# Modulation work spread over more stages, and split activations moved by a part of 128 bytes, in a two-layer hybrid flow step on one Trainium2 core

## The chip, the cores and the metric

The kernel runs on one core of one Trainium2 chip. The metric is the device time of one execution in microseconds (us). TensorE does the matrix products, VectorE and ScalarE the elementwise work, SyncE issues all DMAs; GpSimd does next to nothing here.

## What is computed

128 context tokens and 256 latent tokens (384 in all, three blocks of 128) pass through two layers of a hybrid backbone, everything in float32. Cut to what matters:

```python
def trunk_layer(x, mod, s0f, s0b, lp):                  # twice, DEPTH = 2
    shift1, scale1, gate1, shift2, scale2, gate2 = jnp.split(mod, 6, axis=-1)
    h = rms_norm(x, lp['g_norm1']) * (1 + scale1) + shift1
    z, xbc, dt_raw, p, u, v, gate_logits = jnp.split(h @ lp['w_in'], offs, axis=-1)
    y_ssd, s_f, s_b = ssd_mixer(z, xbc, dt_raw, s0f, s0b, ...)   # conv, SiLU, chunked scan both ways
    y_pool = pool_mixer(p, lp['w_pool'], lp['pool_scale'])       # windows of 2, 4, 8, 16 tokens
    y_gmlp = chunk_gmlp(u, v, lp['g_sgu'], lp['w_spatial'], lp['b_spatial'])  # v = rms_norm(v) first
    g_a, g_b, g_c = jnp.split(jax.nn.sigmoid(gate_logits), N_BRANCH, axis=-1)
    merged = (g_a * (y_ssd @ lp['w_br_ssd']) + g_b * (y_pool @ lp['w_br_pool'])
              + g_c * (y_gmlp @ lp['w_br_gmlp']))
    x = x + gate1 * (merged @ lp['w_out'])
    h2 = rms_norm(x, lp['g_norm2']) * (1 + scale2) + shift2
    f_gate, f_up = jnp.split(h2 @ lp['w_ffn_in'], 2, axis=-1)
    x = x + gate2 * ((jax.nn.silu(f_gate) * f_up) @ lp['w_ffn_out'])
...
    mod_ctx = (jax.nn.silu(c_ctx) @ w_ada[l] + b_ada[l]).reshape(1, 1, -1)   # adaLN modulation
    mod_lat = (jax.nn.silu(c) @ w_ada[l] + b_ada[l])[:, None, :]
```

D_MODEL is 1024, the SSD has 2048 channels in 32 heads, the FFN 2816. At the end comes one more RMSNorm, and the final scan states of the context tokens are returned too.

## The kernel before

**Split products.** TensorE works on a rounded form of float32 (`fp32r`). Each operand is split in a high part, rounded, and a low part, the rest; a product is three matmuls, high by high, high by low, low by high. There are two forms. In `mm3` (lines 165 to 167) the stationary operand is a 128x128 piece of the weights (`whi`, `wlo`), and the activations of all 384 tokens move; a unit of 1024 inputs is 24 such matmuls. In `opt_b`, called through `block_b` and `tiles_b` (lines 454 to 456), the stationary operand is a 128-token block of the activations and 512 columns of the weights move. The activations lie split in SBUF: `hthi`/`htlo` (the normalized input of all projections of a stage), `yh`/`yl` (the SSD's output), and pairs `ah`/`al` that `hl()` hands out from 16 buffers (pooled, mixed and gMLP values, which move; the merged values and the FFN's products, which are stationary in `opt_b`).

**Weights as a stream.** The class `Flow` holds a list of units in program order, each with its weight chunks. A chunk is 512 KB, one DMA into one of six raw buffers (128x1024). For a weight ScalarE casts it to `whi` (line 115), VectorE subtracts to get `wlo` (line 116); three chunks are split ahead. TensorE's order is the order of the list. On the other engines a scheduler orders the instructions by the priorities of program order, the split casts put a little ahead.

**Modulation.** The adaLN vectors of sections 2 to 5 of layer 0 and all six of layer 1 are 80 chunks ("ada") in the same stream. They need no TensorE: `ada` (line 289) has VectorE multiply each raw chunk by a row of SiLU(c), once for the context and once for the latent row, and sum along it (line 299, tile `ajunk`). The rows `crow` come from `silu_rows` (line 280), which stands at the end of the first front. After a section's eighth chunk `ada_end` transposes the result.

**Stages, per layer.** Front: the gMLP's `v` is projected, its statistics taken, and it is kept in HBM. SSD: dt, convolutions over B, C and x (`conv_unit`, tiles `cin`, `ca`, `th`, `bt`, `ct`), z, 16 pairs of heads with their scan, and as fillers between them the gMLP's `u` and the merge gates. Mixers: the order string `6745g23g1g0gAgB` names eight pool units (digits), late gate units (g) and the two group products of the pool's weights (A, B); then 8 units of the pool branch (brp) with the spatial gating between them, 8 of the gMLP branch (brg). Back: the output projection (out), the second norm, the first FFN units (fb), gate and up units (fi), and the FFN's output (fo) in two halves. The modulation chunks stand thus in the stream: 8 in each SSD stage, one after every second step in the mixers (16 per layer), 24 in the FFN of layer 0 and 8 in that of layer 1. In the mixers `mix_open` loads `v` back (`k<-vd`), and VectorE multiplies it by its reciprocal root mean square (tile `k`, factor `ssy`).

Of the kernel before, what the change touches and what calls it, by code (L numbers as in the profile page):

```python
# [19 lines left out]
D = 1024  # L20
# [20 lines left out]
HL = 16  # L41
WPRI = 1
# [13 lines left out]

ADA_S, ADA_M, ADA_F = 2, 2, 1
# [65 lines left out]
class Net:  # L123
# [67 lines left out]
    def build(self):  # L191
# [20 lines left out]
        self.hthi = b.tile([128, KT, TOK], F32R, name="hthi")  # L212
        self.htlo = b.tile([128, KT, TOK], F32R, name="htlo")
# [66 lines left out]
    def silu_rows(self):  # L280

        for n in range(2):
            c = self.crow[:, n, :]
            th = self.t(self.pool, "k4", [128, D], 4)
            self.act(th, c, ACTF.Tanh, scale=0.5)
            self.stt(c, th, 1.0, c, ALU.add, ALU.mult)
            self.ts(c, c, 0.5, ALU.mult)

    def ada(self, l, sec):

        hold = {}
# [12 lines left out]

        return [([("ada", l, sec, k)], step(k)) for k in range(KT)]

    def take(self, us):

        if us:
            self.flow.add(*us.pop(0))  # L310
# [169 lines left out]
    def front0(self):  # L480
# [84 lines left out]
        F.add([], self.silu_rows)  # L565
# [10 lines left out]
    def ssd(self, l):  # L576
# [4 lines left out]
        ada = self.ada(l, 2)  # L581

# [8 lines left out]
        for g in range(4):  # L591
# [7 lines left out]
            for t in range(4 * g, 4 * g + 4):  # L599
# [5 lines left out]
                if (t + 1) % ADA_S == 0:  # L605
                    self.take(ada)
# [9 lines left out]
        while ada:  # L616
            self.take(ada)
# [314 lines left out]
    def mixers(self, l):  # L932
# [3 lines left out]
        ada, count = self.ada(l, 3) + self.ada(l, 4), [0]  # L936

        def more():
            count[0] += 1
            if count[0] % ADA_M == 0:  # L940
                self.take(ada)

# [117 lines left out]
    def branch(self, l, br, c, w, src):  # L1060
# [13 lines left out]
        h = self.mg[c] = self.hl()  # L1074
# [37 lines left out]
    def back(self, l):  # L1112
# [19 lines left out]
        ada = self.ada(l, 5) + (self.ada(l + 1, 0) + self.ada(l + 1, 1) if l + 1 < DEPTH else [])  # L1132

# [14 lines left out]
        for half, kn in enumerate((6, 5)):  # L1148
            for f in range(at, at + 2 * kn - (0 if half else 2)):
# [3 lines left out]
                for _ in range(ADA_F + (f % 4 == 0)):  # L1153
                    self.take(ada)
                self.main([("fi", l, NF + f)], lambda w, f=f: self.ffn_up(l, f, w))
            at = 12
            if half == 0:
                F.add([], lambda: setattr(self, "rows", self.gate_rows(l, 1)))
            for q in range(2):
                spans = (1,) * (kn - KL) + (KL,) if half and q else (1,) * kn  # L1160
# [3 lines left out]
                self.block_b([("fo", l, q, r) for r in range(r0, r0 + kn)], spans, lambda k, r0=r0: self.fa[2 * r0 + k], after, mid, last)  # L1164
# [28 lines left out]
    def ffn_up(self, l, f, w):  # L1193
# [4 lines left out]
        h = self.fa[f] = self.hl()  # L1198
# [174 lines left out]
```

## Time and profile before

| | |
|---|---|
| median of 3 runs (lowest, highest) | 1877.2 us (1876.57, 1879.7) |
| profiled execution, its span | 1876.65 us, 1874.9 us |
| TensorE busy | 1831.0 us (98%) |
| VectorE busy | 1451.4 us (77%) |
| ScalarE busy | 965.1 us (51%) |
| DMA, mean | 182 GB/s, 341 MB |

By the trace the stages lie at: front of layer 0 until 67 us, its SSD 67 to 490, mixers 490 to 636, out and fb to 690, FFN to 955; layer 1: front to 1000, SSD to 1407, mixers to 1551, out to 1605, FFN to 1866, end 1875. A matmul's record lasts longer than the distance to the next one, since they are pipelined: a rate is read from start to start. A wait is the idle time of an engine just before an instruction, put down to what released it.

### The profile page before, as it was taken

How to read it: one execution, taken by the hardware profiler on the slowest of the kernel's cores; microseconds unless marked ns; L12 is line 12 of the kernel's file. 1: busy time of each engine (PE TensorE's matmuls, PEld its weight loads, DVE VectorE, ACT ScalarE, POOL GpSimd, SP SyncE). 2: the span in 40 equal slices, each digit the busy share in tenths (PEclk: the TensorE clock that was granted, in tenths of full speed). 3: DMA queues.
4: the chain of work that ended last, by engine and by line, in shares of the span. 5: the costliest groups of instructions: out<-in, count | busy, mean ns of one | idle time of the engine just before them, and what ended most of it. 6: DMA issues, size and time to landing. Idle time of an engine off the chain costs nothing.

```text
span 1874.9 us, 28980 instructions
## 1 busy us (share of the span) xinstructions
PE 1831.0 (98%) x10724; PEld 1730.5 (92%) x10724; DVE 1451.4 (77%) x2899; ACT 965.1 (51%) x1910; POOL 0.2 (0%) x4
## 2 busy tenths in 40 slices
PE   7989999999999999999999999999999899999998
PEld 4889999999999979989889999999999898998997
DVE  4699979998888787486458989799979887843545
ACT  4677767675342353323355977675833334432332
POOL 0000000000000000000000000000000000000000
PEclk9999999999999999999999999999999999999999
DMA  8756464644766655556445646455457674554431
GB/s 332 248 189 219 150 200 130 210 139 136 262 210 221 213 160 186 170 192 200 124 166 193 211 165 198 149 174 181 135 172 247 222 254 135 192 172 131 124 124 45
DMA packets 112293, 341.15 MB, mean 182 GB/s; under 512 B 12948, under 2 KB 38420, under 8 KB 112024
## 3 DMA queue, kind: packets, MB, share of 16 engines
q1 hardware_dynamic: 112152, 339.30, 55.8%
q8 instruction: 84, 1.38, 0.3%
q14 instruction: 57, 0.47, 0.1%
HBM read 314.38 MB, written 24.87 MB: 181 GB/s over the span
## 4 chain that ended last, share of the span: by engine, by line
PE 82%; DVE 11%; DMA 5%; issue 2%; ACT 1%; SPq 0%; DVEq 0%; ACTq 0%
PE ps_mm L165 19%; PE ps_mm L166 19%; PE ps_mm L167 19%; PE ps_mm L456 5%; PE ps_mm L455 5%; PE ps_mm L454 5%; DMA raw<-w 3%; PE ps_y L875 3%; DVE ajunk L299 2%; DVE wlo L116 2%; DVE ptree L147 1%; DMA k<-vd 1%; PE ps_st L840 1%; DVE t L150 1%; DVE accx L147 1%
## 5 line engine op out<-in xcount | busy, mean ns | idle before, releaser
L115 ACT CAST whi<-raw 128x1024 fp32r<-128x1024 f32 x394 | 412.9, 1050 | 535.6 <-PE ps_mm L166 224.0
L165 PE MATMUL ps_mm<-hthi,whi 128*128 128x384 f32 x1936 | 663.0, 342 | 1.4 <-ACT arg L144 1.4
L116 DVE TENSOR_TENSOR wlo<-raw,whi 128x1024 fp32r<-128x1024 f32 x394 | 481.5, 1223 | 231.8 <-ACT whi L115 227.5
L167 PE MATMUL ps_mm<-hthi,wlo 128*128 128x384 f32 x1936 | 655.0, 338 | 2.1 <-DVE wlo L116 2.1
L166 PE MATMUL ps_mm<-htlo,whi 128*128 128x384 f32 x1936 | 655.0, 338 | 0.0
L165 PEld LDWEIGHTS ps_mm<-hthi,whi 128*128 128x128 f32 x1936 | 364.8, 188 | 4.1 <-ACT arg L144 1.8
L167 PEld LDWEIGHTS ps_mm<-hthi,wlo 128*128 128x128 f32 x1936 | 364.4, 188 | 2.5 <-DVE wlo L116 2.5
L166 PEld LDWEIGHTS ps_mm<-htlo,whi 128*128 128x128 f32 x1936 | 364.7, 188 | 0.3
L299 DVE CUSTOM_DVE_ANT_0 ajunk<-raw,crow 128x1024 bf16<-128x1024 f32 x160 | 195.8, 1224 | 53.9 <-DMA raw<-w 53.0
L456 PE MATMUL ps_mm<-whi,al 128*128 128x512 f32 (+1 forms) x360 | 140.3, 390 | 0.0
L454 PE MATMUL ps_mm<-whi,ah 128*128 128x512 f32 (+1 forms) x360 | 140.0, 389 | 0.0
L455 PE MATMUL ps_mm<-wlo,ah 128*128 128x512 f32 (+1 forms) x360 | 139.2, 387 | 0.0
L150 DVE SCALAR_TENSOR_TENSOR ca<-cin,cw,ca 128x388 f32<-128x388 f32 x192 | 118.8, 619 | 2.1
L165 PE MATMUL ps_mm<-ah,whi 128*128 128x384 f32 x288 | 100.3, 348 | 11.3 <-ACT ah L159 8.1
L159 ACT CAST ah<-t 128x384 fp32r<-128x384 f32 x72 | 36.8, 511 | 124.9 <-DVE t L150 64.8
L166 PE MATMUL ps_mm<-al,whi 128*128 128x384 f32 x288 | 99.0, 344 | 1.1 <-DVE al L147 1.1
L167 PE MATMUL ps_mm<-ah,wlo 128*128 128x384 f32 x288 | 98.5, 342 | 0.0
L165 PE MATMUL ps_mm<-yh,whi 128*128 128x384 f32 x256 | 86.8, 339 | 0.0
L166 PE MATMUL ps_mm<-yl,whi 128*128 128x384 f32 x256 | 86.1, 336 | 0.0
L167 PE MATMUL ps_mm<-yh,wlo 128*128 128x384 f32 x256 | 86.1, 336 | 0.0
L455 PEld LDWEIGHTS ps_mm<-wlo,ah 128*128 128x128 f32 x360 | 67.6, 188 | 14.7
L456 PEld LDWEIGHTS ps_mm<-whi,al 128*128 128x128 f32 x360 | 67.6, 188 | 14.4
(234 smaller groups left out, 2454.3 us busy)
## 6 DMA issues: line engine op xcount, KB each, us to landing
raw<-w SPq DMA_DIRECT2D x474, 512.0 KB, 4.1
fb<-fsd SPq DMA_DIRECT2D x32, 768.0 KB, 4.8
thd<-spill SPq DMA_DIRECT2D x48, 192.0 KB, 2.4
spill<-thd SPq DMA_DIRECT2D x48, 192.0 KB, 4.5
araw<-wa SPq DMA_DIRECT2D x16, 512.0 KB, 5.7
s<-s SPq DMA_DIRECT2D x32, 128.0 KB, 2.2
so<-so SPq DMA_DIRECT2D x32, 128.0 KB, 2.5
k<-gd SPq DMA_DIRECT2D x8, 512.0 KB, 5.4
```

The source lines that it names most:

```text
L115: self.nc.scalar.copy(out=hi, in_=raw)
L116: self.nc.vector.tensor_tensor(out=lo, in0=raw, in1=hi.bitcast(F32), op=ALU.subtract)
L147: self.nc.vector.tensor_tensor(out=out, in0=a, in1=b, op=op)
L150: self.nc.vector.scalar_tensor_tensor(out=out, in0=a, scalar=s, in1=b, op0=op0, op1=op1)
L165: mm(out, lhsT=whi, rhs=xhi, start=first, stop=False)
L166: mm(out, lhsT=whi, rhs=xlo, start=False, stop=False)
L167: mm(out, lhsT=wlo, rhs=xhi, start=False, stop=last)
L299: self.nc.vector.tensor_tensor_reduce(out=junk, in0=raw, in1=self.crow[:, n, :], scale=1.0, scalar=0.0, op0=ALU.mult, op1=ALU.add, accum_o ...
L454: mm(out, lhsT=xh[:, ts], rhs=hi[:, ws], start=(kk == 0), stop=False)
L455: mm(out, lhsT=xh[:, ts], rhs=lo[:, ws], start=False, stop=False)
L456: mm(out, lhsT=xl[:, ts], rhs=hi[:, ws], start=False, stop=(kk == kn - 1))
L875: mm(o, lhsT=lt, rhs=rt, start=(n == 0), stop=(n == steps - 1))
```

## The change

The change has five parts.

1. **Modulation chunks.** One queue, `adaq`, holds all 80 in order, and stages take from it. In the SSD of layer 0 it is 12 instead of 8, in that of layer 1 8 as before; in the mixers of layer 0 one at each of the five `g` steps and one after each brg unit, 13 instead of 16; in those of layer 1 8, none before brg; in the FFN of layer 0 35 instead of 24, also between the spans of fo (`between`); in that of layer 1 4 instead of 8. Loads and products are as many as before.
2. **SiLU rows.** They are computed in the first SSD stage, one ahead of each of the first two z units. The multiplication by 0.5 goes into the scale of the `ajunk` products.
3. **Scaling of `v`** goes from VectorE to ScalarE (Copy with a scale).
4. **Start addresses.** `hthi` and `htlo` become parts of one tile that begin 28 floats into it; an `ah`/`al` tile gets 416 columns of which 384 from column 12 on are used where they move (`AO`), from column 0 where they are stationary (`SO`). In the built program `hthi` and `htlo` started at 64 bytes modulo 128 and now start at 48; the moving `ah`/`al` started at 0 and now start at 48; the stationary `ah`/`al` stay at 0, `yh`/`yl` at 32, `whi`/`wlo` at 64.
5. **Output tiles.** The two halves of a block's output get a tile each; the stores are the same.

TensorE's instructions are the same, in the same order but for the four transposes of finished modulation sections.

```diff
+HO, AO, SO, AW = 28, 12, 0, 416
...
-ADA_S, ADA_M, ADA_F = 2, 2, 1
...
-        self.hthi = b.tile([128, KT, TOK], F32R, name="hthi")
-        self.htlo = b.tile([128, KT, TOK], F32R, name="htlo")
+
+        self.hthl = b.tile([128, 2 * KT * TOK + 32], F32R, name="hthl")
+        self.hthi, self.htlo = (self.hthl[:, HO + n * KT * TOK:HO + (n + 1) * KT * TOK].rearrange("p (k t) -> p k t", t=TOK) for n in range(2))
...
-    def silu_rows(self):
-
-        for n in range(2):
-            c = self.crow[:, n, :]
-            th = self.t(self.pool, "k4", [128, D], 4)
-            self.act(th, c, ACTF.Tanh, scale=0.5)
-            self.stt(c, th, 1.0, c, ALU.add, ALU.mult)
-            self.ts(c, c, 0.5, ALU.mult)
+    def silu_row(self, n):
+
+        c = self.crow[:, n, :]
+        th = self.t(self.pool, "ef", [128, 4, 256], 1).rearrange("p a b -> p (a b)")
+        self.act(th, c, ACTF.Tanh, scale=0.5)
+        self.stt(c, th, 1.0, c, ALU.add, ALU.mult)
...
-                    self.nc.vector.tensor_tensor_reduce(out=junk, in0=raw, in1=self.crow[:, n, :], scale=1.0, scalar=0.0,
+                    self.nc.vector.tensor_tensor_reduce(out=junk, in0=raw, in1=self.crow[:, n, :], scale=0.5, scalar=0.0,
...
+    def take(self, n=1):
+
+        for _ in range(n):
+            if self.adaq:
+                self.flow.add(*self.adaq.pop(0)[1:])
...
             self.front0()
+            self.adaq = [u for n in range(DEPTH) for sec in range(0 if n else 2, 6) for u in self.ada(n, sec)]
...
-                if (t + 1) % ADA_S == 0:
-                    self.take(ada)
+                if l == 0 and t < 2:
+                    F.add([], lambda t=t: self.silu_row(t))
+                self.take((t % 2 == 1) + (l == 0 and t % 4 == 2))
...
             if step == "g":
                 G()
+                self.take(l == 0)
...
-            more()
...
             self.main([("brg", l, c)], lambda w, c=c: self.branch(l, 2, c, w, self.gm))
-            more()
-        while ada:
-            self.take(ada)
-
-    def hl(self):
-        return (self.t(self.pool, "ah", [128, TOK], HL, F32R), self.t(self.pool, "al", [128, TOK], HL, F32R))
+            self.take()
+        self.ada_until(l, 4)
+
+    def hl(self, o=AO):
+        return (self.t(self.pool, "ah", [128, AW], HL, F32R)[:, o:o + TOK], self.t(self.pool, "al", [128, AW], HL, F32R)[:, o:o + TOK])
...
-            self.ts(v, v, self.vr[i], ALU.mult)
+            self.act(v, v, ACTF.Copy, scale=self.vr[i])
...
-                for _ in range(ADA_F + (f % 4 == 0)):
-                    self.take(ada)
                 self.main([("fi", l, NF + f)], lambda w, f=f: self.ffn_up(l, f, w))
+                self.take()
...
-        y = self.t(self.pool, "yo", [128, D], 2)
+        y0 = self.t(self.pool, "bsp" if i % 2 else "wst", [128, 512], 1)
+        y1 = self.t(self.pool, "yo", [128, 512], 2)
```

Two places show what moves on the engines. The first is ScalarE at the start of the first SSD stage, before: `res` is the last copy of the front, `arg` the first step of dt, `cin` the first input of a convolution, `crow` the conditioning rows.

```order
L477 COPY res<-ps_mm 128x512 x2
L115 CAST whi<-raw 128x1024 x2
L144 ACTIVATE k_743<-crow 128x1024
L144 ACTIVATE k_747<-crow 128x1024
L115 CAST whi<-raw 128x1024
L144 ACTIVATE arg<-ps_mm,cp 64x384
L144 ACTIVATE ea<-cp 64x1
L742 COPY cin_759<-ps_mm 128x128
L144 ACTIVATE W<-arg 64x384
```

The same place of ScalarE in the changed kernel:

```order
L485 COPY res<-ps_mm 128x512 x2
L115 CAST whi<-raw 128x1024
L144 ACTIVATE arg<-ps_mm,cp 64x384
L144 ACTIVATE ea<-cp 64x1
L746 COPY cin_750<-ps_mm 128x128
L144 ACTIVATE W<-arg 64x384
L747 COPY cin_750<-ps_mm 128x256
L144 ACTIVATE W<-W 64x384
L144 ACTIVATE ca<-cin_750,cw 128x388
L115 CAST whi<-raw 128x1024
L746 COPY cin_751<-ps_mm 128x128
L747 COPY cin_751<-ps_mm 128x256
```

The two tanh over `crow` and two weight casts that stood ahead of `arg` now come behind it; the first tanh follows one row after the piece shown.

The second place is VectorE in the pool stage of the mixers of layer 1, before: `ptree` holds the running sums of a pool unit, `t` its result, `al` the low part that the group product takes, `ajunk` a modulation product.

```order
L150 SCALAR_TENSOR_TENSOR t_15514<-ptree,pin_15154 128x256
L299 ISA ajunk,mod_15274<-raw,crow 128x1024
L299 ISA mod_15274 128x1
L147 TENSOR_TENSOR al<-t_15514,ah 128x384
L299 ISA ajunk,mod_15274<-raw,crow 128x1024
L299 ISA mod_15274 128x1
L147 TENSOR_TENSOR ptree<-pin_15153 128x415
L116 TENSOR_TENSOR wlo<-raw,whi 128x1024
L147 TENSOR_TENSOR ptree<-ptree,edge 128x1 x2
```

The same place of VectorE in the changed kernel:

```order
L150 SCALAR_TENSOR_TENSOR t_15573<-ptree,pin_15232 128x256
L116 TENSOR_TENSOR wlo<-raw,whi 128x1024
L147 TENSOR_TENSOR al<-t_15573,ah 128x384
L116 TENSOR_TENSOR wlo<-raw,whi 128x1024
L147 TENSOR_TENSOR ptree<-pin_15231 128x415
L147 TENSOR_TENSOR ptree<-ptree,edge 128x1 x2
L150 SCALAR_TENSOR_TENSOR t_15651<-ptree,pin_15231 128x128
```

The modulation products between the pool's steps are gone there; what stays between them is the weight split.

## Rows read from the trace of the kernel before

**Rows 1.** The page: busy time of the engines, and the chain's shares by engine

```profile
PE 1831.0 (98%) x10724; PEld 1730.5 (92%) x10724; DVE 1451.4 (77%) x2899; ACT 965.1 (51%) x1910; POOL 0.2 (0%) x4
...
PE 82%; DVE 11%; DMA 5%; issue 2%; ACT 1%; SPq 0%; DVEq 0%; ACTq 0%
```

**Rows 2.** The page's groups: line, engine, operation, count, busy us, mean ns, idle before

```profile
L165 PE MATMUL ps_mm<-hthi,whi 128*128 128x384 f32 x1936 | 663.0, 342 | 1.4 <-ACT arg L144 1.4
...
L165 PE MATMUL ps_mm<-ah,whi 128*128 128x384 f32 x288 | 100.3, 348 | 11.3 <-ACT ah L159 8.1
```

**Rows 3.** Timeline of TensorE, FFN of layer 0: start us, us, operation

```profile
851.31 0.34 PE L165 MATMUL ps_mm<-hthi,whi 128*128 128x384 f32 x1
...
906.23 0.34 PE L165 MATMUL ps_mm<-hthi,whi 128*128 128x384 f32 x1
```

**Rows 4.** Timeline of TensorE, end of the first SSD stage

```profile
473.70 0.34 PE L165 MATMUL ps_mm<-yh,whi 128*128 128x384 f32 x1
...
488.27 0.34 PE L165 MATMUL ps_mm<-yh,whi 128*128 128x384 f32 x1
```

**Rows 5.** Timeline of TensorE, gMLP branch of layer 0

```profile
606.31 0.34 PE L165 MATMUL ps_mm<-ah,whi 128*128 128x384 f32 x1
...
631.47 0.34 PE L165 MATMUL ps_mm<-ah,whi 128*128 128x384 f32 x1
```

**Rows 6.** Timeline of TensorE, last FFN output, 256 columns of weights moving

```profile
1861.16 0.28 PE L454 MATMUL ps_mm<-whi,ah 128*128 128x256 f32 x1
...
1866.26 0.28 PE L454 MATMUL ps_y<-whi,ah 128*128 128x256 f32 x1
```

**Rows 7.** Waits of TensorE: what waited for what, us in total, times, longest

```profile
PE ps_mm L165 <- ACT ah L159: 8.1, 2, 4.7
PE ps_tr L779 <- DVE ct L150: 4.8, 1, 4.8
...
PE ps_tr L399 <- DVE k L154: 4.1, 4, 1.6
PE ps_mm L165 <- DVE t L150: 3.2, 3, 1.6
...
PE ps_mm L165 <- ACT arg L144: 1.4, 1, 1.4
```

**Rows 8.** Busy time by stretch: length, engines' busy us, granted clock, DMA

```profile
100.00:104.00 4.00, 3.49 (x12) 3.20 (x13) 3.97 (x8) 0.00 (x0) 0.00 (x0) 0.50 0.55 141
...
103.00:490.00 387.00, 387.00 (x2546) 378.48 (x2545) 346.38 (x740) 267.45 (x611) 0.00 (x0) 1.00 0.56 177
490.00:546.00 56.00, 52.13 (x293) 51.41 (x293) 53.72 (x126) 22.30 (x41) 0.00 (x0) 0.99 0.76 249
546.00:552.00 6.00, 6.00 (x21) 6.00 (x22) 3.19 (x5) 1.59 (x3) 0.00 (x0) 0.54 0.77 257
690.00:950.00 260.00, 260.00 (x1367) 243.74 (x1366) 170.94 (x257) 87.60 (x122) 0.00 (x0) 1.00 0.55 177
1019.00:1407.00 388.00, 388.00 (x2556) 379.47 (x2556) 344.13 (x733) 268.74 (x610) 0.00 (x0) 1.00 0.55 179
1407.00:1463.00 56.00, 50.63 (x285) 49.91 (x284) 53.30 (x125) 21.15 (x40) 0.00 (x0) 0.97 0.76 248
1463.00:1467.00 4.00, 4.00 (x15) 4.00 (x16) 2.63 (x4) 0.96 (x2) 0.00 (x0) 0.59 0.74 237
```

**Rows 9.** Timeline of ScalarE and VectorE at the start of the first SSD stage

```profile
80.61 2.01 ACT L144 ACTIVATE k<-crow 128x1024 f32<-128x1024 f32 x2
...
81.86 2.35 DVE L150 SCALAR_TENSOR_TENSOR crow<-k,crow 128x1024 f32<-128x1024 f32 x2
```

**Rows 10.** The page's group of the modulation products

```profile
L299 DVE CUSTOM_DVE_ANT_0 ajunk<-raw,crow 128x1024 bf16<-128x1024 f32 x160 | 195.8, 1224 | 53.9 <-DMA raw<-w 53.0
```

**Rows 11.** Timeline of VectorE, `v` scaled at the start of the mixers

```profile
502.52 0.75 DVE L154 TENSOR_SCALAR k<-k,ssy 128x1024 f32<-128x1024 f32 x1 [1.55 <-DMA k<-vd]
```

**Rows 12.** Timeline of VectorE, the last output

```profile
1870.47 0.48 DVE L150 SCALAR_TENSOR_TENSOR yo<-accx,ssy,k 128x256 f32<-128x256 f32 x1
```

More of the change, by code (lines that the diff above doesn't have):

```diff
@@ L303, in step, with ada_until @@
             return fn
[L305 to L310, printed above, removed]
+        return [((l, sec), [("ada", l, sec, k)], step(k)) for k in range(KT)]
+    def take(self, n=1):
+        for _ in range(n):
+            if self.adaq:
+                self.flow.add(*self.adaq.pop(0)[1:])
+    def ada_until(self, l, sec):
+        while self.adaq and self.adaq[0][0] <= (l, sec):
+            self.take()
     def ada_end(self, l, sec, m):
@@ L456, in opt_b, with block_b @@
                 mm(out, lhsT=xl[:, ts], rhs=hi[:, ws], start=False, stop=(kk == kn - 1))
-    def block_b(self, keys, spans, src, after=None, mid={}, halves=None):
+    def block_b(self, keys, spans, src, after=None, mid={}, halves=None, between=None):
         hold, kn, at = {}, 2 * len(keys), 0
@@ L468, in block_b @@
             self.flow.add(keys[at:at + sp], lambda *w, at=at, a=a: self.tiles_b(get, 512, w, 2 * at, kn, src, at, mid, a, halves))
+            if between and n < len(spans) - 1:
+                between()
             at += sp
@@ L564, in front0 @@
         F.add([], self.masks)
-        F.add([], self.silu_rows)
     def front(self, l):
@@ L935, in mixers @@
         self.tick = 0
[L936 to L940, printed above, removed]
-                self.take(ada)
         def P(c):
@@ L1073, in branch @@
         self.tt(t, a, t, ALU.add)
-        h = self.mg[c] = self.hl()
+        h = self.mg[c] = self.hl(SO)
         self.act(h[0], t, ACTF.Copy, scale=0.5)
@@ L1152, in back @@
                     F.add([], lambda: self.ffn_turn(l))
-                for _ in range(ADA_F + (f % 4 == 0)):
-                    self.take(ada)
                 self.main([("fi", l, NF + f)], lambda w, f=f: self.ffn_up(l, f, w))
+                self.take()
             at = 12
             if half == 0:
+                self.ada_until(l, 5)
                 F.add([], lambda: setattr(self, "rows", self.gate_rows(l, 1)))
             for q in range(2):
+                if half and q and l + 1 < DEPTH:
+                    self.ada_until(l + 1, 1)
                 spans = (1,) * (kn - KL) + (KL,) if half and q else (1,) * kn
@@ L1163, in back @@
                 after, last = fo_end(q, half)
-                self.block_b([("fo", l, q, r) for r in range(r0, r0 + kn)], spans, lambda k, r0=r0: self.fa[2 * r0 + k], after, mid, last)
+                self.block_b([("fo", l, q, r) for r in range(r0, r0 + kn)], spans, lambda k, r0=r0: self.fa[2 * r0 + k], after, mid, last, self.take)
     def ffn_first(self, l, i, ps):
@@ L1176, in ffn_turn @@
         for f in range(2):
-            h = self.fa[f] = self.hl()
+            h = self.fa[f] = self.hl(SO)
             tp = self.ps("tr")
@@ L1197, in ffn_up @@
         self.stt(g, g, 0.5, ps[:, 0:TOK], ALU.mult, ALU.mult)
-        h = self.fa[f] = self.hl()
+        h = self.fa[f] = self.hl(SO)
         self.split(h[0], h[1], g)
@@ L1224, in store @@
         nc, io = self.nc, self.io
-        y = self.t(self.pool, "yo", [128, D], 2)
-        self.stt(y[:, c0:c0 + n], self.x[:, i, c0:c0 + n], r, self.gf[:, c0:c0 + n], ALU.mult, ALU.mult)
-        self.act(y[:, 0:512], self.xg[i], ACTF.Copy, scale=r)
+        y0 = self.t(self.pool, "bsp" if i % 2 else "wst", [128, 512], 1)
+        y1 = self.t(self.pool, "yo", [128, 512], 2)
+        self.stt(y1[:, c0 - 512:c0 - 512 + n], self.x[:, i, c0:c0 + n], r, self.gf[:, c0:c0 + n], ALU.mult, ALU.mult)
+        self.act(y0, self.xg[i], ACTF.Copy, scale=r)
         if c0 > 512:
-            self.ts(y[:, 512:c0], self.xg[i, 1], r, ALU.mult)
-        for h in range(2):
-            nc.sync.dma_start(out=io["yo"][i, :, h * 512:(h + 1) * 512], in_=y[:, h * 512:(h + 1) * 512])
+            self.ts(y1[:, 0:c0 - 512], self.xg[i, 1], r, ALU.mult)
+        for h, y in enumerate((y0, y1)):
+            nc.sync.dma_start(out=io["yo"][i, :, h * 512:(h + 1) * 512], in_=y)
 @with_exitstack
```

5 lines of the change are left out of this document (removed).

## The prediction

> **What bounds the kernel now.** I read the page first: in the span of 1874.9 us TensorE is busy 98%, and the chain that ended last is TensorE's for 82%, VectorE's for 11% and DMA's for 5% [rows 1]. So two things can shorten the run: fewer ns from one matmul to the next, or shorter stretches in which TensorE stands. Transfers and ScalarE matter only where they feed one of these.
>
> For the first I read the groups by line and then single matmuls. The weight products with 384 token columns moving are the mass: 3 × 1936 = 5808 matmuls move `hthi`/`htlo`, 3 × 288 = 864 move `ah`/`al` [rows 2]. A record's 337 ns is its latency, not its price; the price is the distance of two starts. For `hthi` I take two starts with 13 full units of 24 matmuls between them: 54.92 us / 312 = 176.0 ns [rows 3]. For `yh` 84 matmuls take 14.57 us = 173.5 ns [rows 4], for `ah` 144 take 25.16 us = 174.7 ns [rows 5]. The three have the same shape, the same kind of stationary weights, and TensorE does not wait in these stretches; what differs is the tile, and where it starts: at 64, 32 and 0 bytes of a 128-byte line (the change section says so). For a fourth reading, 45 matmuls with 256 moving columns take 5.10 us = 113.3 ns [rows 6]; per column that is 0.443 ns, so 384 columns at this rate would take 170.0 ns.
>
> For the second I read what TensorE waited for. The sum of the named waits is small, but five rows touch the change: 8.1 us in two waits for `ah`, 4.8 us for `ct`, 1.4 us for `arg`, 3.2 us for `t`, 4.1 us for `k` [rows 7]. Then the table by stage [rows 8]: VectorE is busy 346 of 387 us in the first SSD stage, 344 of 388 in the second, and 53.7 and 53.3 of 56 us in the two pool stages of the mixers, at whose ends the `ah` waits stand. Behind each long wait the granted clock is down: 0.50 in 100–104, 0.54 in 546–552, 0.59 in 1463–1467, which is the level of 1.2 GHz or a mixture with it, and 0.97 to 1.00 elsewhere.
>
> **The change, part by part.**
>
> *Start address of the moving tiles.* Of `hthi`/`htlo` it goes from 64 to 48, of the moving `ah`/`al` from 0 to 48; `yh`, the weights and the stationary activations of the other form (but `hthi` in two short stages) keep theirs. No row shows a tile at 48. The bounds: 170.0 ns, the per-column rate of the 256-column rows [rows 6], and 176.0, no change [rows 3]. 48 lies between 32, which gives 173.5, and 64, which gives 176.0 or, with 256 columns, 170.0; I take the middle of 173.5 and 170.0, 171.7 ns. Then 5808 × (176.0 − 171.7) = 25 us and 864 × (174.7 − 171.7) = 2.6 us, 27.6 together. The SSD stages hold about half of the 5808 matmuls, some 12.5 us of that, and there VectorE is at 90% and would have to follow; I let a third of it, 4 us, be lost. **−24 us** (0 to −34 inside these bounds).
>
> *SiLU rows and the start of SSD.* Now two tanh of 2.01 us together on ScalarE and two multiplications of 2.35 us together on VectorE stand ahead of dt's `arg` [rows 9]. They go behind it, so dt and the convolution start that much earlier. What it can give is 1.4 us (`arg`), 4.8 us (`ct`), and the slow clock behind it: 4 us at 0.50 are 2 us [rows 7, 8]; 8.2 in all. `th`, ahead of `ct`, still stands behind a spill on ScalarE, so I take **−7 us** (−1 to −8).
>
> *Modulation chunks.* Each is one 512 KB load and two products of 1.22 us on VectorE, 160 products and 195.8 us in all [rows 10], as many as before. In the pool stages, first layer: 13 products before, 10 in the change; second layer: 13 before, none. VectorE is 95% busy there [rows 8], so 13 × 1.22 = 16 us fewer are more than the whole wait in layer 1, and three fewer plus the three scalings of `v` at 0.75 us and the 1.55 us idle before one [rows 11] are 7.5 us against the 8.1 − 4.7 = 3.4 us of the `ah` wait in layer 0. The two waits give 8.1; the slow clock behind them 6 × 0.46 = 2.8 and 4 × 0.41 = 1.6; 12.5 in all. **−12 us** (0 to −12.5). The waits for `t` and `k` sit among later products that mostly stay: −1 of their 7.3 (0 to −3).
>
> What these products displace: the first SSD stage gets 24 instead of 20, and the two SiLU multiplications: 4.9 + 2.35 = 7.2 us on 346 of 387; the FFN of layer 0 gets 22 more, 27 us on 171 of 260 [rows 8]. The FFN has room, so I put it at nothing; the cover is the 89 us in which VectorE idles there, and without it the cost is what exceeds. In SSD the room is 41 us on average but not everywhere, so **+3 us** (0 to +8).
>
> *Scaling `v` on ScalarE.* ScalarE takes 1.0 us for 128x1024 [rows 9], three of them, in a stage where it is busy 22 of 56 us [rows 8]: nothing. If one waits for its load as VectorE does (1.55 us), the weight casts queued behind it on ScalarE are late by that; three raw buffers of lead cover it. Bound: +1.5.
>
> *Output tiles apart.* Two tiles instead of one, the same stores of the same size; nothing, at most the 0.48 us of the last product on either side [rows 12].
>
> The sum: −24 − 7 − 12 − 1 + 3 = −41. The profiled execution took 1876.65 us, 0.55 under the median of the runs, so 1835.7 + 0.55, rounded **1836 us**.
>
> **The rivals.**
>
> *(a) The address does nothing.* The differences of [rows 3 to 6] could come from what else runs in those stages. For it: all three readings are in other stages. Against it: the `hthi` stretch lies in the FFN, where VectorE and the transfers are less busy than in the mixers' stretch with `ah`, and is still the slowest. Then the other terms, −17, remain: 1860 us. The Trainium skill, page "SBUF — State Buffer", section "Who interferes with whom", says that TensorE has two independent read ports and never waits on another engine; by that the gap between 176.0 and 173.5 ns can't come from other engines, which the order of these rows agrees with, and by itself it says nothing of an operand's own address.
>
> *(b) The address gives all there is.* If 48 reaches 168 ns, somewhat under the 256-column rate, 5808 × 8 + 864 × 6.7 = 52 us go, less 6 in SSD: 1876.65 − 46 − 17 + 0.55 = 1814. Against it: no stretch among the rows lies under the rate of 170.0. The Trainium skill, page "TensorE: Matmul & The Clock Gate", section "Back-to-back issue gap", has N/2.4 + 2.5 ns, 162.5 for 384 columns; by it 5808 × 13.5 = 78 us could go, an estimate of about 1775. The rows disagree with it as it stands: 113.3 against its 109.2 at 256 columns, 176.0 against 162.5 at 384.
>
> *(c) VectorE becomes the bound in SSD.* Spread chunks and a quicker TensorE meet at 346 + 7 of 387 − 6 us. For it: 93% on average and the products not evenly spread [rows 8]. Then the SSD share of the first term (12.5 us) is lost and 8 us are added: 1836 + 8.5 + 5 = 1850.
>
> *(d) Slower.* The new address costs more instead of less. The other terms give −17, so it turns slower where a matmul costs 17/6672 = 2.5 ns more than now, at 178.5. For it: 48 is no multiple of 32, and all the tiles of the rows start at one. If it lay twice as far over 176.0 as `yh` lies under it, at 181 ns, 5808 × 5 + 864 × 6.3 = 34 us are added: 1876.65 + 34 − 17 + 0.55 = 1894. Against it: no stretch of the rows lies over 176.0 at full clock.
>
> **How the numbers follow.** The forecast's own mechanism, 1822 to 1848: 0.45. (a) 0.18, (b) 0.13, (c) 0.18, (d) 0.04, slower for some other reason 0.02. The likeliest is 1836. From 1814 to 1864 the range holds the forecast, (c), (a), and (b) as far as 168 ns; about 2 in 10 lie outside: (b) beyond that, (d), and (a) with some of the waits kept. A measurement of this kernel tells about 0.2%, 3.8 us, from no change. Slower by more is (d) and the rest, 0.05; within, (a) with all waits staying, 0.03; faster 0.92.
>
> **What would show it.** In the profile of the changed kernel: the start-to-start distance of `hthi` and `ah` matmuls well under 175 in the FFN and in the mixers, `yh` still at 173.5; no wait for `ct` of 4.8 us; no wait for `ah` in layer 1, a shorter one in layer 0, and granted clock near 1 at 546–552 and 1463–1467; new waits for `wlo` or `x` tiles in the first SSD stage if (c) holds. I am wrong in the main term if `hthi` stands at 176 in the FFN, where nothing else limits it, and in the second if the `ah` waits stay though the products are gone.

## The result and the profile after

The changed kernel takes 1848.62 us (median of 4 runs, 1848.01 to 1849.57) against 1878.45 us for the kernel before; the ratio is 0.9839, 95% interval 0.9821 to 0.9857. That is 30 us less, where 41 were forecast: inside the range, at its slower half, and 0.6 us beyond the 1822 to 1848 that the prediction gave to its own mechanism. By the number alone rival (c), 1850, lies nearer, so the stages have to decide. The profiled execution took 1849.57 us with a span of 1847.5 us, 27.4 us under the span of before.

The page again first, busy time and chain, to be laid beside [rows 1]:

```profile
PE 1815.8 (98%) x10724; PEld 1712.7 (93%) x10724; DVE 1449.0 (78%) x2891; ACT 968.8 (52%) x1916; POOL 0.2 (0%) x4
...
PE 88%; DVE 6%; DMA 3%; issue 2%; ACT 1%; SPq 0%; DVEq 0%; ACTq 0%
```

VectorE's share of the chain fell from 11% to 6%: TensorE waits less for it. To see where the time went, I take the start of the same matmul in both traces at each stage's border (but for four transposes the matmuls correspond one to one) and subtract:

| stretch, by the start in the trace before | before, us | after, us | difference |
|---|---|---|---|
| 67.1: dt, first convolutions | 36.2 | 26.9 | −9.3 |
| 103.3: rest of the SSD, layer 0 | 386.7 | 383.4 | −3.3 |
| 490.0: mixers, layer 0 | 146.1 | 136.5 | −9.7 |
| 636.1: output projection, norm, fb | 54.1 | 56.2 | +2.2 |
| 690.2: FFN, layer 0 | 259.8 | 265.2 | +5.4 |
| 950.0: end of FFN, front of layer 1, first SSD units | 69.0 | 69.2 | +0.2 |
| 1019.0: rest of the SSD, layer 1 | 388.1 | 384.3 | −3.8 |
| 1407.1: mixers, layer 1 | 144.0 | 134.9 | −9.1 |
| 1551.2: output projection, norm, fb | 54.1 | 54.7 | +0.6 |
| 1605.2: FFN, layer 1 | 260.8 | 259.5 | −1.3 |

The three places with a wait gave all they had; the FFN of layer 0 became longer. The rate of the weight products answers to [rows 3]: the same 312 matmuls in the timeline of TensorE after,

```profile
837.72 0.33 PE L165 MATMUL ps_mm<-hthl,whi 128*128 128x384 f32 x1
...
891.80 0.33 PE L165 MATMUL ps_mm<-hthl,whi 128*128 128x384 f32 x1
```

54.08 us, 173.3 ns each instead of 176.0. For `ah`, to compare with [rows 5], 144 matmuls:

```profile
584.75 0.33 PE L165 MATMUL ps_mm<-ah,whi 128*128 128x384 f32 x1
...
610.03 0.34 PE L165 MATMUL ps_mm<-ah,whi 128*128 128x384 f32 x1
```

25.28 us, 175.6 ns instead of 174.7: nothing gained. Over the 216 matmuls of the same branch in layer 1 it is 175.6 ns instead of 173.7: a loss, and `ah` at 0 had not had one rate in both layers before. TensorE's waits after, beside [rows 7] (what waited for what, us in total, times, longest):

```profile
PE ps_tr L404 <- DVE k L154: 5.1, 2, 2.6
...
PE ps_mm L460 <- DVE res L147: 3.9, 1, 3.9
...
PE ps_mm L167 <- DVE wlo L116: 2.6, 1, 2.6
...
PE ps_tr L783 <- DVE ct L150: 0.2, 1, 0.2
```

The waits for `ah`, `t` of the mixers and `arg` are gone, the one for `ct` is 0.2 us. One is new: 3.9 us for `res`. By stretch, in the columns of [rows 8], the corresponding stretches in the same order:

```profile
92.00:96.00 4.00, 3.83 (x25) 3.51 (x24) 3.94 (x9) 1.81 (x3) 0.00 (x0) 1.00 0.39 145
94.00:478.00 384.00, 383.32 (x2550) 374.65 (x2550) 357.31 (x758) 266.45 (x614) 0.00 (x0) 1.00 0.59 187
478.00:530.00 52.00, 51.83 (x298) 51.26 (x297) 46.24 (x111) 25.29 (x44) 0.00 (x0) 1.00 0.75 248
530.00:536.00 6.00, 6.00 (x36) 6.00 (x35) 4.16 (x6) 3.29 (x6) 0.00 (x0) 1.00 0.36 120
671.00:936.00 265.00, 260.57 (x1367) 241.99 (x1366) 199.36 (x305) 88.00 (x123) 0.00 (x0) 0.99 0.61 197
...
1390.00:1440.00 50.00, 49.83 (x286) 49.26 (x286) 36.53 (x91) 24.51 (x43) 0.00 (x0) 1.00 0.61 197
1440.00:1444.00 4.00, 4.00 (x25) 4.00 (x24) 2.58 (x4) 2.41 (x4) 0.00 (x0) 1.00 0.45 134
```

(Columns: TensorE, its weight loads, VectorE, ScalarE, GpSimd, then granted clock, share of the DMA engines, GB/s.) The granted clock is 1.00 at all three places where it was 0.50 to 0.59: the wait ahead of it is gone, so the slow stretch behind it too. VectorE, 95% busy in the pool stages before, is at 89% in layer 0 and 73% in layer 1. In the FFN of layer 0 TensorE is now idle for 4.4 us though VectorE is busy only 199 of 265 us. Its timeline there shows why (start, duration, and in brackets the idle time before an instruction and what ended it):

```profile
783.10 1.23 DVE L298 CUSTOM_DVE_ANT_0 ajunk<-raw,crow 128x1024 bf16<-128x1024 f32 x1 [1.16 <-DMA raw<-w]
...
784.37 1.22 DVE L298 CUSTOM_DVE_ANT_0 ajunk<-raw,crow 128x1024 bf16<-128x1024 f32 x1
...
785.52 1.22 DVE L116 TENSOR_TENSOR wlo<-raw,whi 128x1024 fp32r<-128x1024 f32 x1
786.66 1.28 DVE L147 TENSOR_TENSOR res<-ps_mm,k 128x512 f32<-128x512 f32 x2
```

Two modulation products and a weight split stand ahead of `res`, which frees the PSUM banks of one FFN output column for the next; the first of them waits 1.16 us for its chunk. TensorE's first matmul of the next column, at 787.39, has stood 3.89 us for `res`.

Behind this wait the granted clock falls, and so it does behind the wait for `k` of the second norm of layer 0, which is now 2.6 us in one piece and was 0.5 and 1.6 us. The changed kernel first, then the same place of e4_ah0 (one of the runs below), which has the same wait of 2.6 us and stays at full clock:

```profile
788.00:792.00 4.00, 4.00 (x12) 3.14 (x11) 4.00 (x6) 0.00 (x0) 0.00 (x0) 0.57 0.55 203
...
660.00:664.00 4.00, 2.75 (x13) 2.37 (x14) 2.75 (x6) 2.47 (x7) 0.00 (x0) 0.77 0.64 163
664.00:668.00 4.00, 4.00 (x16) 3.16 (x15) 1.84 (x5) 1.56 (x4) 0.00 (x0) 0.80 0.26 103
```

```profile
660.00:664.00 4.00, 3.48 (x19) 3.00 (x20) 2.41 (x7) 2.72 (x7) 0.00 (x0) 1.00 0.59 193
664.00:668.00 4.00, 4.00 (x19) 3.20 (x18) 3.14 (x6) 2.70 (x4) 0.00 (x0) 1.00 0.11 45
```

What a slow stretch costs is its length times the share of the clock that is missing: 4 × 0.43 = 1.7 us behind `res`, 4 × 0.23 + 4 × 0.20 = 1.7 us behind `k`. The second one and the 0.5 us of longer wait are the 2.2 us by which the stretch around the norm grew; in e4_ah0 and e2_rest that stretch takes 54.3 us.

### The profile page after: what moved, and what is told of

Same layout as the page of the kernel before. It is cut to its first block, busy times and chain, and to the rows that moved or that the text cites. A ratio compares the mean times of both kernels' runs of the same rounds, so it can differ in the third digit from the quotient of the medians.

```text
span 1847.5 us, 28977 instructions
## 1 busy us (share of the span) xinstructions
PE 1815.8 (98%) x10724; PEld 1712.7 (93%) x10724; DVE 1449.0 (78%) x2891; ACT 968.8 (52%) x1916; POOL 0.2 (0%) x4
## 4 chain that ended last, share of the span: by engine, by line
PE 88%; DVE 6%; DMA 3%; issue 2%; ACT 1%; SPq 0%; DVEq 0%; ACTq 0%
PE ps_mm L165 21%; PE ps_mm L166 21%; PE ps_mm L167 21%; PE ps_mm L461 5%; PE ps_mm L460 5%; PE ps_mm L462 5%; PE ps_y L879 3%; DMA raw<-w 3%; DVE wlo L116 1%; DVE ajunk L298 1%; PE ps_st L844 1%; PE ps_tr L826 1%; PE ps_mm L1079 1%; PE ps_mm L553 1%; PE ps_tr L511 0%
## 5 line engine op out<-in xcount | busy, mean ns | idle before, releaser
L165 PE MATMUL ps_mm<-hthl,whi 128*128 128x384 f32 x1936 | 656.3, 339 | 0.0
L167 PE MATMUL ps_mm<-hthl,wlo 128*128 128x384 f32 x1936 | 651.3, 336 | 2.6 <-DVE wlo L116 2.6
L166 PE MATMUL ps_mm<-hthl,whi 128*128 128x384 f32 x1936 | 651.0, 336 | 0.0
L167 PEld LDWEIGHTS ps_mm<-hthl,wlo 128*128 128x128 f32 x1936 | 364.1, 188 | 3.0 <-DVE wlo L116 3.0
L165 PEld LDWEIGHTS ps_mm<-hthl,whi 128*128 128x128 f32 x1936 | 364.3, 188 | 2.3 <-issue 1.5
L166 PEld LDWEIGHTS ps_mm<-hthl,whi 128*128 128x128 f32 x1936 | 364.2, 188 | 0.3
L460 PEld LDWEIGHTS ps_mm<-whi,ah 128*128 128x128 f32 x360 | 68.0, 189 | 20.5 <-DVE res L147 4.3
L462 PEld LDWEIGHTS ps_mm<-whi,al 128*128 128x128 f32 x360 | 68.0, 189 | 15.5
```

The source lines that it names most:

```text
L165: mm(out, lhsT=whi, rhs=xhi, start=first, stop=False)
L166: mm(out, lhsT=whi, rhs=xlo, start=False, stop=False)
L167: mm(out, lhsT=wlo, rhs=xhi, start=False, stop=last)
L460: mm(out, lhsT=xh[:, ts], rhs=hi[:, ws], start=(kk == 0), stop=False)
L462: mm(out, lhsT=xl[:, ts], rhs=hi[:, ws], start=False, stop=(kk == kn - 1))
```

## The experiments

The theory after the comparison: (1) the start address of the moving tile sets the rate of the weight products; (2) the start of SSD and the mixers lost their waits because work was taken from ahead of them; (3) the chunks between the FFN's output spans make the new wait; (4) the new pitch of `ah` costs something. The rivals are in the expectations. On the chips of these runs the kernel before had medians from 1875.76 to 1878.45 us, so 2 or 3 us between two kernels measured on different chips are not certain; the traces tell such differences by stage. In the edits, lines that are left out are marked by `...`.

**e1_h48.** The kernel before, `hthi`/`htlo` moved alone.

```diff
+HO = 28
...
-        self.hthi = b.tile([128, KT, TOK], F32R, name="hthi")
-        self.htlo = b.tile([128, KT, TOK], F32R, name="htlo")
+        self.hthl = b.tile([128, 2 * KT * TOK + 32], F32R, name="hthl")
...
```

> The kernel before with one part of the change: hthi and htlo start at 48 instead of 64 bytes modulo 128 (the later tiles move by 128 bytes), ah and al stay. Theory 1 (the start address of the moving tile sets the rate): hthi goes from 176.0 to 173.3 ns from start to start in the FFN of layer 0, as in the changed kernel, 5808 x 2.65 = 15 us, of which VectorE lets perhaps 3 us not through in SSD: about 1866 us against 1878; the waits for ct and ah stay. Rival (the rate of the changed kernel comes from its other stages' load, not from the address): hthi stays at 176 and the time at 1878.

Measured: 1863.41 us (1862.74 to 1867.25) against 1876.89 of the kernel before on the same chip, ratio 0.9931 (0.9919 to 0.9943). The 312 matmuls of the FFN of layer 0 in its trace:

```profile
845.21 0.34 PE L167 MATMUL ps_mm<-hthl,whi 128*128 128x384 f32 x1
...
899.28 0.34 PE L167 MATMUL ps_mm<-hthl,whi 128*128 128x384 f32 x1
```

54.07 us, 173.3 ns. Its waits are those of before:

```profile
PE ps_mm L167 <- ACT ah L161: 9.0, 2, 4.6
PE ps_tr L781 <- DVE ct L152: 4.8, 1, 4.8
```

So this part alone makes 13.5 us, as theory 1 has it. (The tiles laid out behind `hthl` move by 128 bytes too; e9 to e12 leave them in place. Line numbers here are two higher than before.) The rest of the SSD took 382.9 and 384.4 us against 386.7 and 388.1: the SSD passed on its share.

**e2_rest.** The changed kernel with part 4 undone.

```diff
-HO, AO, SO, AW = 28, 12, 0, 416
+HO, AO, SO, AW = 28, 0, 0, 384
...
-        self.hthl = b.tile([128, 2 * KT * TOK + 32], F32R, name="hthl")
...
+        self.hthi = b.tile([128, KT, TOK], F32R, name="hthi")
+        self.htlo = b.tile([128, KT, TOK], F32R, name="htlo")
```

> The changed kernel with part 4 undone: hthi and htlo back at 64, ah and al back at 0 and at their old pitch. Theory 1: hthi back at 176, 15 us more, and the 512-column matmuls back at their old rate (they became 2 to 3 ns slower in the changed kernel, about 3 us): 1860 to 1862 us against 1848.6. Rival: the address does nothing, 1849.

Measured: 1858.83 us (1855.18 to 1860.7), 10 us over the changed kernel, ratio to before 0.9906 (0.9892 to 0.9919). In its trace:

```profile
836.26 0.34 PE L165 MATMUL ps_mm<-hthi,whi 128*128 128x384 f32 x1
...
891.17 0.34 PE L165 MATMUL ps_mm<-hthi,whi 128*128 128x384 f32 x1
```

54.91 us, 176.0 ns again. The rival is out from both sides. The gain of the address within the change is smaller than in e1_h48 because the move of `ah` takes some back (e4_ah0).

**e3_fo.** The changed kernel without chunks between the FFN's output spans.

```diff
-                self.take()
+                self.take(1 if f % 4 == 0 else 2)
...
-                self.block_b([...], spans, lambda k, r0=r0: self.fa[2 * r0 + k], after, mid, last, self.take)
+                self.block_b([...], spans, lambda k, r0=r0: self.fa[2 * r0 + k], after, mid, last)
```

> The changed kernel with no modulation chunk between the spans of the FFN's output: the 15 chunks that stood there come after the up units, two after three of four units instead of one, 35 in all as before. Theory 3 (the wait of 3.9 us for res at 787 us comes from residuals queued on VectorE behind modulation products that wait for their loads): the wait goes, the FFN of layer 0 is 5 to 6 us shorter, 1843 us. Rival (35 chunks in this stage are too many wherever they stand): another wait takes its place in the gate and up units, 1849 us or more.

Measured: 1843.63 us (1842.89 to 1845.42), 5.0 under the changed kernel by the medians and 2.6 by the ratios to before (0.9825 against 0.9839). In the traces the FFN of layer 0 takes 258.7 us instead of 265.2. Its waits hold no `res`, and in the FFN of layer 0 TensorE is never idle, with VectorE as busy as in the changed kernel (199 there):

```profile
665.00:930.00 265.00, 265.00 (x1395) 246.27 (x1394) 200.78 (x312) 91.63 (x129) 0.00 (x0) 1.00 0.62 197
```

Theory 3: it is the place of the chunks, not their number.

**e4_ah0.** The changed kernel with `ah`/`al` at the old offset and pitch.

```diff
-HO, AO, SO, AW = 28, 12, 0, 416
+HO, AO, SO, AW = 28, 0, 0, 384
```

> The changed kernel with ah and al back at offset 0 and a pitch of 1536 bytes, hthi and htlo still at 48. In the changed kernel ah showed no gain (174.7 before, 175 after) and the 512-column matmuls with ah stationary lost 2 to 3 ns each. Theory 4 (the pitch of 1664 bytes costs this): 512 columns back at 229 ns, some 1050 x 2.5 = 2.6 us less, ah at 174.7: 1846 us. Rival (the loss comes from the other tiles having moved by 128 bytes, or from the modulation work beside them): no change, 1849 us.

Measured: 1843.76 us (1841.31 to 1846.24), 4.9 under the changed kernel, more than expected. In the profiled execution the wait for `res` was 2.7 us instead of 3.9, with no slow clock behind it. What goes with the pitch is seen where nothing waits, in the FFN's output of layer 1, where the stationary `ah` starts at 0 of its tile in both: 112 matmuls with 512 columns between these two starts. Timeline of TensorE of the changed kernel,

```profile
1688.28 0.40 PE L461 MATMUL ps_mm<-wlo,ah 128*128 128x512 f32 x1
...
1714.27 0.40 PE L462 MATMUL ps_mm<-whi,al 128*128 128x512 f32 x1
```

and of the kernel that has both costs taken back (e8_fo_ah0, below), with the pitch of before:

```profile
1678.29 0.39 PE L461 MATMUL ps_mm<-wlo,ah 128*128 128x512 f32 x1
...
1703.92 0.40 PE L462 MATMUL ps_mm<-whi,al 128*128 128x512 f32 x1
```

25.99 us or 232.1 ns against 25.63 us or 228.8 ns; e4_ah0 itself has 228.9 there too. 3.2 ns over some 1050 such matmuls are 3.4 us. The rest of the 4.9 is not shown: the shorter wait is no proof of it, since that wait is 2.5 us in e7_v_dve too, at the new pitch, and without any wait for `res` the pitch of before still gives 4.6 us (e8_fo_ah0 against e3_fo, on different chips). So moving `ah` was a loss: no gain where it moves, and a cost where it is stationary. Whether the pitch does it, or the tiles that it shifts, was not separated.

**e5_scan.** The changed kernel with slices 388 floats apart.

```diff
-HO, AO, SO, AW = 28, 12, 0, 416
+HO, AO, SO, AW, HP = 28, 12, 0, 416, 388
...
-        self.hthl = b.tile([128, 2 * KT * TOK + 32], F32R, name="hthl")
+        self.hthl = b.tile([128, 2 * KT * HP + 32], F32R, name="hthl")
...
```

> The changed kernel with 388 instead of 384 floats from one 128-row slice of hthi (and of htlo) to the next: slice k then starts 16 k bytes further on in the 128-byte line, at 48, 64, 80, 96, 112, 0, 16, 32 for k = 0 to 7, so one trace has the rate at eight addresses. Theory 1, sharpened (multiples of 64 bytes cost 176 ns, the rest 173.3): slices 1 and 5 stand at 176, the six others at 173.3. Rival (only the distance between addresses of consecutive matmuls matters, or the address of the whole tile): all eight alike. Another rival (48 is the one good place, by luck): slice 0 alone is quick.

Measured, one run: 1857.01 us. Averaged over the units of an uninterrupted stretch (480 matmuls from 814 us on), the three matmuls of a slice take 171.1, 173.0, 174.4, 177.0, 176.9, 173.6, 176.4 and 175.3 ns each at 48, 64, 80, 96, 112, 0, 16 and 32. The first matmuls of slices 1 and 4 of one unit, and of slices 0 and 1 of the next:

```profile
839.77 0.34 PE L165 MATMUL ps_mm<-hthl,whi 128*128 128x384 f32 x1
...
841.34 0.34 PE L165 MATMUL ps_mm<-hthl,whi 128*128 128x384 f32 x1
...
843.45 0.34 PE L165 MATMUL ps_mm<-hthl,whi 128*128 128x384 f32 x1
843.96 0.34 PE L165 MATMUL ps_mm<-hthl,whi 128*128 128x384 f32 x1
```

From 843.45 slice 0, at 48, takes 0.51 us; from 839.77 eight slices take 4.19 us, 174.6 ns a matmul. None of the three expectations holds in full, though slice 0 is the quickest: 64 and 0, the multiples of 64, are not the slow ones, eight addresses are not alike, and 48 is not alone. It also has a flaw: `hthi` and `htlo` stand 128 bytes apart modulo 256 here and 0 in the other kernels. Hence e9 to e12, with one address at a time.

**e6_silu.** The kernel before with the SiLU rows moved alone.

```diff
-        F.add([], self.silu_rows)
...
+                if l == 0 and t < 2:
+                    F.add([], lambda t=t: self.silu_row(t))
```

> The kernel before with part 2 alone (SiLU rows in the first SSD stage). If the start of SSD waits for the tanh and the products ahead of dt, the waits for arg and ct and the slow clock behind them go, 8 to 9 us: 1868 us against 1877. Rival (another wait, for the weights' low parts or for th behind a spill, takes their place): 1874 to 1877.

Measured: 1867.43 us (1864.82 to 1871.72) against 1875.76, ratio 0.9955 (0.9937 to 0.9973): 8.3 us. The stretch from 67 to 103 us has its 27.0 us, no wait for `arg` or `ct` is left, and those of the mixers stay:

```profile
PE ps_mm L165 <- ACT ah L159: 7.5, 2, 4.8
...
PE ps_mm L165 <- DVE t L150: 2.4, 3, 1.4
```

**e7_v_dve.** The changed kernel with `v` scaled on VectorE.

```diff
-            self.act(v, v, ACTF.Copy, scale=self.vr[i])
+            self.ts(v, v, self.vr[i], ALU.mult)
```

> The changed kernel with v scaled on VectorE as before. If ScalarE has the room and VectorE of layer 0's pool stage needs the 2.3 us and the wait for the load, part of the ah wait of layer 0 comes back: 1849 to 1852 us. If the removed modulation products alone were enough: 1848.6, no wait for ah.

Measured: 1848.87 us (1844.14 to 1850.01), no difference from the changed kernel; no wait for `ah`, and from the start of the mixers of layer 0 to the first group product it takes the same 50.4 us as the changed kernel, against 54.7 before. Part 3 is worth nothing here once the modulation products are gone. (Its profiled execution, the quickest of the four, has a wait for `res` of 2.5 us with no slow clock behind it; in the changed kernel these were 3.9 us and 1.7 us lost. So the price of the chunks between the spans is probably not the same in every execution.)

**e8_fo_ah0.** The edits of e3_fo and e4_ah0 together.

> The changed kernel with two of its parts taken back that the runs so far show as costs: no modulation chunk between the spans of the FFN's output, and ah and al at offset 0 with the old pitch. Alone they gave 5.0 and 4.9 us, but the second had already halved the wait for res, so together 7 to 9 us: 1840 to 1842 us. Rival (both gains are the same wait): 1843.5.

Measured: 1839.04 us (1837.93 to 1839.56), ratio to before 0.9801 (0.9788 to 0.9815), 9.6 us under the changed kernel and 9.8 under e7_v_dve, which was measured on the same chip: the fastest version of this study, and the two costs are separate ones.

**e9 to e12.** The same kernel with only the start of `hthi`/`htlo` moved, at 32, 0, 16 and 112 bytes modulo 128 instead of 48. The edits are

```diff
-HO, AO, SO, AW = 28, 0, 0, 384
+HO, AO, SO, AW = 24, 0, 0, 384
```

for e9_at32, and 16, 20 and 12 in the place of 24 for e10_at0, e11_at16 and e12_at112.

> The kernel without chunks between the FFN output's spans and with ah and al as before (1839.0 us), hthi and htlo at 32 instead of 48 bytes modulo 128; no other tile moves. Theory A (each address has its own rate, as in the scan's slices): yh stood at 32 with 173.5 ns, the scan's slice 7 with 175.3: 173.3 to 175.3 in the FFN, 1839 to 1850 us. Rival B (in a run of matmuls at one address the rate locks at 173.3 wherever the address is no multiple of 64; the scan's differences came from the steps between slices): 173.3 and 1839 us.

> The same with hthi and htlo at 0 modulo 128. Theory A: the scan's slice 5 took 173.6 and ah at 0 took 173 to 175: 173.3 to 174.7 ns, 1839 to 1846 us. Rival B (multiples of 64 are the slow ones): 176 ns, 1839 + 15 = 1854 us.

> The same with hthi and htlo at 16 modulo 128. Theory A: the scan's slice 6 took 176.4 ns: 5808 x 3 = 18 us more than 1839, less in SSD, about 1855 us. Rival B: 173.3 ns and 1839 us.

> The same with hthi and htlo at 112 modulo 128. Theory A: the scan's slice 4 took 176.9 ns: 1839 + 20, about 1857 us. Rival B: 173.3 ns and 1839 us.

192 matmuls of the FFN of layer 1, timeline of TensorE, first of e9_at32:

```profile
1739.26 0.34 PE L165 MATMUL ps_mm<-hthl,whi 128*128 128x384 f32 x1
...
1773.18 0.34 PE L165 MATMUL ps_mm<-hthl,whi 128*128 128x384 f32 x1
```

of e10_at0:

```profile
1728.79 0.34 PE L165 MATMUL ps_mm<-hthl,whi 128*128 128x384 f32 x1
...
1762.07 0.34 PE L165 MATMUL ps_mm<-hthl,whi 128*128 128x384 f32 x1
```

of e11_at16:

```profile
1729.56 0.34 PE L165 MATMUL ps_mm<-hthl,whi 128*128 128x384 f32 x1
...
1763.16 0.34 PE L165 MATMUL ps_mm<-hthl,whi 128*128 128x384 f32 x1
```

and of e12_at112:

```profile
1733.23 0.34 PE L165 MATMUL ps_mm<-hthl,whi 128*128 128x384 f32 x1
...
1766.83 0.34 PE L165 MATMUL ps_mm<-hthl,whi 128*128 128x384 f32 x1
```

| `hthi` at, modulo 128 | kernel | ns, FFN layer 1 | median us | ratio to before |
|---|---|---|---|---|
| 48 | e8_fo_ah0 | 173.3 | 1839.04 | 0.9801 |
| 0 | e10_at0 | 173.3 | 1843.51 | 0.9825 (0.9810 to 0.9839) |
| 16 | e11_at16 | 175.0 | 1845.16 | 0.9832 (0.9816 to 0.9848) |
| 112 | e12_at112 | 175.0 | 1849.50 | 0.9858 (0.9843 to 0.9872) |
| 32 | e9_at32 | 176.7 | 1855.81 | 0.9892 (0.9877 to 0.9906) |

Both theories fall as rules: 32 is the slowest though `yh`, also at 32, keeps its 173.5 in the same run and the scan had it in the middle; 16 and 112 are slower than 48, but in this stretch not by 3 ns; 0 has the good rate. And the rate in the table is not the whole of it: in e11_at16 and e12_at112 it changes from one stretch to another, with the tile at the same place. Two stretches of 192 matmuls of e12_at112, in the gate and up units of layer 0 and of layer 1:

```profile
710.33 0.34 PE L165 MATMUL ps_mm<-hthl,whi 128*128 128x384 f32 x1
...
743.61 0.34 PE L165 MATMUL ps_mm<-hthl,whi 128*128 128x384 f32 x1
...
1604.46 0.34 PE L165 MATMUL ps_mm<-hthl,whi 128*128 128x384 f32 x1
...
1638.38 0.34 PE L165 MATMUL ps_mm<-hthl,whi 128*128 128x384 f32 x1
```

33.28 us and 33.92 us, 173.3 and 176.7 ns, where the table has 175.0. Each of these five kernels has 44 stretches of at least 40 such matmuls, up to 480, with no other matmul or wait between. Read from the 25th matmul on, each stretch holds one of three levels, 173.3, 175.0 or 176.7 ns within 0.1: with the tile at 48 and at 0 all 44 have the first, at 32 all 44 the last; at 16 there are 23 of the first and 21 of the second; at 112 they are 5, 32 and 7. So the rate holds within a stretch, and that much rival B had right, but not at one level. That is also why 112 is 4.3 us slower than 16 with the same figure in the table.

So that the start of this one tile moves the time is shown by five kernels that differ in nothing else; but it doesn't fix the rate alone, and by what rule it acts is open. And e10_at0, as quick as e8_fo_ah0 in the 384-column matmuls, lost 4.5 us elsewhere: its 512-column matmuls take 26.13 us in the stretch shown under e4_ah0, 233.3 ns, though there only the start of `hthi` differs and `hthi` takes no part in it. This is so in the FFN's output of both layers (some 690 matmuls, 3 us); in the output projection of the same run matmuls of the same form have 228.9. The rest is in its profiled execution a slow clock at the front of layer 1 that e8_fo_ah0 has not.

## Why the prediction was right, and where its sizes were off

**The address, −24.** Right in kind (e1_h48, e2_rest), mis-sized: 13.5 us. I took 171.7 ns, between the `yh` row and the per-column rate of the 256-column rows; the rate was 173.3, that of `yh`, and 5808 × 2.7 = 15.5 us. So the 256-column rate was no guide for 384, and to read a rate off the address by lying between two others was no argument: 32 and 0 don't rank in `hthi` as they did in `yh` and `ah` (e9_at32, e10_at0). The third that I let the SSD lose was not lost: both long SSD stretches became shorter by the 1490 × 2.6 ns or nearly that (3.3 and 3.8 of 3.9; 3.9 and 3.7 in e1_h48). The 2.6 us for `ah` were a loss of 4.9 us instead (e4_ah0). I had priced the stationary use at nothing because its start stays at 0, and did not look at the pitch.

**The start of SSD, −7.** Right, a little small: 8.3 us alone (e6_silu), in that stretch of its trace 9.2, over my bound of 8.2. `th` behind a spill did not hold `ct` back, and the slow clock was priced too low, here and in the mixers: I took windows that cut it. With it whole, before:

```profile
97.00:105.00 8.00, 4.49 (x16) 4.20 (x17) 7.94 (x15) 0.53 (x1) 0.00 (x0) 0.57 0.35 97
544.00:552.00 8.00, 6.93 (x22) 6.53 (x23) 5.19 (x9) 2.49 (x5) 0.00 (x0) 0.57 0.79 263
1459.00:1467.00 8.00, 4.89 (x16) 4.50 (x17) 6.41 (x14) 1.86 (x4) 0.00 (x0) 0.57 0.78 264
```

8 × 0.43 = 3.4 us at each place, where I had 2, 2.8 and 1.6.

**The mixers, −12 and −1.** Too small by about 4. The stages of both layers lost 9.7 and 9.1 us, of which the 312 and 304 `hthi` matmuls explain 0.8 each; some 17 remain. All of the `ah` waits, the slow clock behind them (2.4 us more than I had) and also the waits for `t`, of which I had counted next to nothing, went. No run has the moved chunks alone: that it was they follows by exclusion, since the waits stay with the address or the SiLU rows alone (e1_h48, e6_silu) and are gone without the address or the scaling of `v` (e2_rest, e7_v_dve). In layer 0 eight of thirteen products are still there between 478 and 530 us, and no wait: a few less were enough.

**More work in SSD, +3.** It costs some 0.5 us, by the difference between the two layers' gains there (3.3 and 3.8) and by the 382.9 us of e1_h48 against 383.4, with VectorE at 357 of 384 us. Rival (c), VectorE as the bound in SSD, did not come about: that the time lies near its 1850 is chance.

**The FFN of layer 0, at nothing.** This step failed. I named 89 us of idle time as cover, but the cover was an average: the products stand in VectorE's order ahead of the residuals, wait for their chunks with all behind them, and TensorE needs the banks that the residuals free. The price was 5.0 us (e3_fo); in the trace of the changed kernel most of it is the wait of 3.9 us for `res` and 1.7 us of slow clock behind it.

**Output tiles, nothing.** From the start of the last matmul to the end it takes 8.4 us before and 8.3 after.

The sum by runs: −13.5 + 4.9 − 8.3 − 17 + 5.0 = −28.9 against a measured −29.8. That it comes so close is in part luck, since each of these medians is uncertain by a microsecond or more. The forecast came within its range because errors of opposite sign met: the address and `ah` gave 15 us less than the 24 forecast and the FFN cost 5, while the waits gave 5 more and the SSD did not cost the 3. Of the rivals, (a) is out by e1_h48 and (b) by the rate after: no uninterrupted stretch of `hthi` matmuls in any of these runs came under 173 ns as a whole. (d) did not come about at 48, but addresses slower than the old one exist: at 32 the rate is 176.7, and that kernel takes 16.8 us more than the one at 48.

The 2.2 us around the second norm of layer 0 and the slow clock behind `res` stood in no term. The same wait of 2.6 us for `k` was followed by a slow stretch in the changed kernel and in e3_fo and e8_fo_ah0 (55.8 to 56.3 us), and not in e2_rest and e4_ah0; what decides it is not shown.

## What to carry to other kernels

Idle time on an engine is no cover by its sum: look at what stands next in that engine's order behind the added instruction, and whether the added instruction itself waits for a load. Work that needs no TensorE belongs where no other engine's next step is waited for, and little of it has to move: in the mixers of layer 0 five products of 1.22 us fewer went with the end of a wait and of the slow clock behind it. Where one kind of matmul is most of the run, read its start-to-start distance by tile: tiles of one shape can differ by 2%, and the start address is worth a measured scan, one address at a time, for moving and stationary tiles apart. Read more than one stretch of each run: at two of five addresses the rate changed within the run. And price a slow clock over the whole stretch in which it is down.

## What the runs showed of the hardware that I had not expected

With 384 moving columns at full granted clock the distance of matmuls stood at 173.3, 175.0 or 176.7 ns through whole uninterrupted stretches, and at 175.5 to 176.5 in the kernel before. With nothing else moved, the tile at 48 or 0 had 173.3 in all of them, at 32 176.7 in all; at 16 some stretches had 173.3 and some 175.0, at 112 all three levels came up. So the start address takes part in it, and something else that changes from one stretch to the next.

The 512-column rate was 228.8 ns with the old pitch of the stationary tiles and 232.1 with the new one, and it stood at 233.3 in the FFN's output of a kernel in which neither these tiles nor the weights had moved. What links the addresses to these rates wasn't settled.

A wait of 2.6 us of TensorE was followed by a stretch at half of the clock, at a loss of 1.7 us, in some executions and not in others.
